# Hybrid encoder layer on one core: late gate products that share a weight unit between two blocks, and mLSTM exponents with a bias

## The chip, the cores and the metric

The kernel runs on one core of one Trainium2 chip. The metric is the device time of one execution in microseconds (us); three executions of the kernel before gave 2991.52, 2993.33 and 2995.25, median 2993.33. A difference under about 0.2% (6 us) can't be told from none.

## The reference, cut to what matters

One encoder layer on 2048 tokens of width 1024, all in float32. Three mixers run on the same normalised input `h`: a bidirectional chunked mLSTM (4 heads), a neighbourhood attention and a cross-attention; sigmoid gates computed from `h` merge them, an output projection and an MLP follow. The change touches the gates and the exponents of the mLSTM:

```python
gates = jax.nn.sigmoid(gate_pre)              # gate_pre = h @ w_in[:, 2576:5648], 3 x 1024 columns
y = (gates[:, :, 0] * (h_m @ w_proj_mlstm) + gates[:, :, 1] * (h_na @ w_proj_na)
     + gates[:, :, 2] * (h_mem @ w_proj_mem))
...
# one mLSTM chunk, one direction, one head; lf, ig: log forget gate and input gate per token
b = jnp.cumsum(lf)
d_log = jnp.where(tril, b[:, None] - b[None, :] + ig[None, :], -jnp.inf)
m_t = jnp.maximum(b + m_st, jnp.max(d_log, axis=-1))
s = (q @ k.T) * jnp.exp(d_log - m_t[:, None])
w_inter = jnp.exp(b + m_st - m_t)
```

The exponent of the chunk's 128 x 128 matrix is a sum of a number per query token (`r = b - m`) and a number per key token (`a = ig - b`).

## The kernel before, in words

Tokens stand in four blocks of 512. Every large product is three matmuls in a shortened float32 format (high by high, high by low, low by high), in the helper `mm3`, lines L232 to L234. In a product of channels by tokens (`ch_group`) a weight unit of 128 channels is the stationary operand, 8 pieces of the inner dimension follow one another, and 512 tokens are the moving columns: 24 matmuls. Weight units come from memory as 512 KB (`wr`, L172), ScalarE takes the high part (L176), VectorE the low part (L177), into one of five buffers `ws`; `take` fetches several units ahead, in the order of the list in `plan`.

- **Phase 1** makes the projections of the four blocks and both attentions; the gates of blocks 2 and 3 too. Its last products are the four of `o` in block 3 (destination `mm`, stationary operand `hT`). Between them the input operand `hT` of block 1 is copied back from memory into the place of block 3's, 128 tokens at a time; the last 128 tokens come in eight pieces (L568).
- **Phase 2**, the mLSTM stage, has 48 gate products left: 24 of block 1, then 24 of block 0 (`late_gates`, `gate`). Each fetches its own weight unit. Between the two blocks `hT` is loaded again (L609), and four ticks pass without a product.
- **Phase 3** merges, projects, and runs the MLP. Its operands are seven planes of one tile `X`.

A *tick* comes after every six matmuls of a gate product. At a tick the mLSTM stream `ml_stream` issues its next step, so the order on TensorE (PE) is written out by hand: six gate matmuls, one small mLSTM step, six gate matmuls. On the other engines a scheduler sets the order by priority; each engine then executes in order, and SyncE (SP) issues all transfers in one queue. The stream starts after 20 ticks. It alternates between the two directions, one chunk of 128 tokens each four ticks. Before the first chunk of a block of 512 tokens, `ml_block` computes that block's rows for one direction in one go: two scans on VectorE (L750, L754), differences, splits (L759 to L767), an exponential, four small transposes (L773). Scans and differences of a direction work on 4 partitions.

A chunk (`ml_chunk`) passes through steps: its loads; the exponents, by one matmul into PSUM (`pd`, L810) whose operands `at` and `rd` are built from the rows by VectorE and GpSimd (L807), an exponential on ScalarE (`de`, L812) and a mask on GpSimd (L814); the products of q and k (L828), masked by `de` into `pt` (L830); transposed keys (L839) and copies for the other direction (`sk`, L832, L841); outputs (`pn`, L863, L866); state update (`pu`, L872, into `C`, L878); and, for the direction that comes second to a chunk, normalisation, transposes `tr` (L905) and storage (`hm`, L907, L908). In the second half of the stage the copies in `sk` replace L828 and L839.

In phase 2 PSUM has two buffers for gate products (`mm`), four for `pn`, and two, called `mx`, that all other small results (`pd`, `psc`, `pk`, `pu`, `tr`) take in turn.

Of the kernel before, what the change touches and what calls it, by code (L numbers as in the profile page):

```python
# [16 lines left out]
ALU = mybir.AluOpType  # L17
# [8 lines left out]
TICKS_2, START_2 = 4, 20  # L26
PAD = 192
# [53 lines left out]
class Body:  # L81
# [176 lines left out]
    def phases(self):  # L258
# [7 lines left out]
        with tc.tile_pool(name="p2", bufs=1) as self.p_a:  # L266
            self.pad(self.p_a, PAD)
            self.ev_bufs = EV[2]
            self.psum(self.phase_2, mm=2, pn=4, mx=2)
        with tc.tile_pool(name="p3", bufs=1) as self.p_a:  # L270
            self.pad(self.p_a, PAD)
            self.ev_bufs = EV[3]
            self.psum(self.phase_3, mm=8)
# [14 lines left out]
    def scratch(self):  # L288
# [16 lines left out]
            w=[[d(f"s_w{i}{b}", [4, TB]) for b in range(NB)] for i in range(2)],  # L305
            hm=[d(f"s_hm{b}", [128, 2, 4, TB]) for b in range(NB)],
# [289 lines left out]
    def gate(self, b, j):  # L596

        p = self.ch_group(self.take(1)[0], self.hT)
# [4 lines left out]
    def late_gates(self, more):  # L603

        while self.gq and more():
            b, j = self.gq.pop(0)
            if j == 0 and b != GATES_2[0]:
                for k in range(0, 8, 2):
                    self.nc.sync.dma_start(self.hT[:, :, k:k + 2].bitcast(F32), self.scr["hT"][b][:, :, k:k + 2])  # L609
                for _ in range(TICKS_2):  # L610
                    self.tick()
            self.gate(b, j)


    def phase_2(self):
        nc, a = self.nc, self.a
        self.ml_consts()
# [6 lines left out]
    def ml_stream(self):  # L624


        for _ in range(START_2):
            yield
        dirs = [list(range(16)), list(range(15, -1, -1))]
        live = [[], []]  # L630
        when = {0: [(2, 0)], 1: [(1, 1), (2, 1), (3, 0)], 2: [(1, 2)], 3: [(3, 0), (1, 3), (0, 1)]}
        d = 0
        while any(dirs) or any(live[0]) or any(live[1]):
            c = dirs[d].pop(0) if dirs[d] else None
            if c is not None and c % 4 == (0, 3)[d]:
                self.ml_block(d, c // 4)
            live[d] = [None if c is None else self.ml_chunk(d, c)] + live[d][:3]
            for tick in range(4):
                for age, _ in when[tick]:
                    if age < len(live[d]) and live[d][age]:  # L640
                        next(live[d][age], None)
                yield
# [32 lines left out]
    def ml_consts(self):  # L675
# [7 lines left out]

        self.bd = t("bd", [36, 4, 128])
        nc.vector.memset(self.bd, 0.0)
        for d in range(2):
            nc.gpsimd.affine_select(out=self.bd, in_=self.bd, compare_op=ALU.not_equal, fill=1.0, base=-32 * d,
                                    pattern=[[-1, 4], [0, 128]], channel_multiplier=1)


        self.at, self.rd, self.rp = {}, {}, {}
        for d in range(2):
            for i in range(2):
                at = self.at[d, i] = t(f"at{d}{i}", [100, TB], F32R)
                rd = self.rd[d, i] = t(f"rd{d}{i}", [100, 4, 128], F32R)
                rp = self.rp[d, i] = t(f"rp{d}{i}", [36, TB])
                for x in (at, rd, rp):
                    nc.gpsimd.memset(x.bitcast(F32), 0.0)
                for k in range(2):
                    nc.vector.tensor_copy(rd[32 * k:32 * k + 4], self.bd[32 * k:32 * k + 4])  # L700
                    nc.vector.tensor_scalar(at[64 + 32 * k:68 + 32 * k], self.reset[32 * k:32 * k + 4], 0.0, 1.0, ALU.mult, ALU.add)
        self.carry = t("carry", [36, 1])
        nc.vector.memset(self.carry, NEG)
        self.packs = []
# [33 lines left out]
    def ml_block(self, d, b):  # L738

        nc = self.nc  # L740
        n = b if d == 0 else 3 - b
        hs = slice(32 * d, 32 * d + 4)
        if d == 0:
            self.packs.append({x: self.row("r_" + x, (36, TB + (x == "m")), bufs=1) for x in "ifbmw"})
        P = {x: y[hs] for x, y in self.packs[n].items()}
        ig, lf, bs, m, w = (P[x] for x in "ifbmw")
        nc.sync.dma_start(ig, self.scr["ig"][4 * d:4 * d + 4, b * TB:(b + 1) * TB])
        nc.sync.dma_start(lf, self.scr["lf"][4 * d:4 * d + 4, b * TB:(b + 1) * TB])
        rev = (lambda x: x[:, ::-1]) if d else (lambda x: x)
        nc.vector.tensor_tensor_scan(rev(bs), self.reset[hs], rev(lf), 0.0, ALU.mult, ALU.add)  # L750
        cm, ce = (m[:, 1:], m[:, 0:1]) if d == 0 else (m[:, :TB], m[:, TB:])
        carry = self.carry[hs]
        nc.vector.tensor_copy(ce, carry)
# [824 lines left out]
```

## Time and profile before

| | us |
|---|---|
| median of three runs | 2993.33 |
| the profiled execution, whole | 2998.03 |
| its span (first to last instruction) | 2996.3 |
| PE busy in the span | 2929.4 (98%) |
| VectorE (DVE), ScalarE (ACT), GpSimd (POOL) busy | 2066.5, 1195.8, 268.8 |
| phase 1, to the last product of `o` | 0 to 946.5 |
| phase 2 and the last gate products | 946.5 to 1377.3 |
| phase 3 | 1377.3 to 2996.3 |

Rows of PE in a timeline show an instruction's start and its modelled length, which overlaps with the next; what an instruction costs is the distance of two starts. A group's idle time is the time in which the engine stood still ahead of it, with what ended the wait.

### The profile page before, as it was taken

How to read it: one execution, taken by the hardware profiler on the slowest of the kernel's cores; microseconds unless marked ns; L12 is line 12 of the kernel's file. 1: busy time of each engine (PE TensorE's matmuls, PEld its weight loads, DVE VectorE, ACT ScalarE, POOL GpSimd, SP SyncE). 2: the span in 40 equal slices, each digit the busy share in tenths (PEclk: the TensorE clock that was granted, in tenths of full speed). 3: DMA queues.
4: the chain of work that ended last, by engine and by line, in shares of the span. 5: the costliest groups of instructions: out<-in, count | busy, mean ns of one | idle time of the engine just before them, and what ended most of it. 6: DMA issues, size and time to landing. Idle time of an engine off the chain costs nothing.

```text
span 2996.3 us, 41916 instructions
## 1 busy us (share of the span) xinstructions
PE 2929.4 (98%) x15028; PEld 2375.1 (79%) x15028; DVE 2066.5 (69%) x3523; ACT 1195.8 (40%) x2198; POOL 268.8 (9%) x423
## 2 busy tenths in 40 slices
PE   8999999999989899999999999999999999999999
PEld 6888888778777677778888888888778888888887
DVE  6676864476654766765688878666675987885665
ACT  6465654355543333342243333533312433334331
POOL 4121200021001323420000000000000000000000
PEclk9999999999999999999999999999999999999999
DMA  8786877876998667788444445766863444466554
GB/s 276 222 275 200 242 231 246 275 215 203 289 283 267 199 202 236 247 275 306 141 132 161 144 149 178 256 195 218 280 209 119 148 151 146 142 223 226 191 185 165
DMA packets 341712, 632.97 MB, mean 211 GB/s; under 512 B 29344, under 2 KB 151008, under 8 KB 341504
## 3 DMA queue, kind: packets, MB, share of 16 engines
q1 hardware_dynamic: 341504, 630.30, 65.5%
q8 instruction: 118, 1.93, 0.3%
q14 instruction: 90, 0.74, 0.1%
HBM read 453.63 MB, written 176.55 MB: 210 GB/s over the span
## 4 chain that ended last, share of the span: by engine, by line
PE 55%; DVE 2%; DMA 2%; issue 1%; ACT 0%; POOL 0%; SPq 0%; DVEq 0%; ACTq 0%; POOLq 0%
PE mm L232 18%; PE mm L233 18%; PE mm L234 18%; PE mm L1341 0%; DMA wr<-in_w_units_dram 0%; DMA hf<-s_hf 0%; DVE h L901 0%; DMA og<-s_o 0%; DVE ev L1497 0%; DVE acc L1490 0%; ACT hf L897 0%; POOL rs L325 0%; DMA X<-s_a 0%; DVE ws L177 0%; DVE h L889 0%
## 5 line engine op out<-in xcount | busy, mean ns | idle before, releaser
L232 PE MATMUL mm<-X,ws 128*128 128x512 f32 x1152 | 455.7, 396 | 0.0
L234 PE MATMUL mm<-X,ws 128*128 128x512 f32 x1152 | 455.4, 395 | 0.0
L233 PE MATMUL mm<-X,ws 128*128 128x512 f32 x1152 | 455.4, 395 | 0.0
L232 PE MATMUL mm<-hT,ws 128*128 128x512 f32 x896 | 375.0, 419 | 8.2 <-DMA hT<-s_hT 4.4
L177 DVE TENSOR_TENSOR ws<-wr,ws 128x1024 fp32r<-128x1024 f32 (+1 forms) x212 | 264.5, 1254 | 136.2 <-ACT ws L176 132.6
L234 PE MATMUL mm<-hT,ws 128*128 128x512 f32 x896 | 353.2, 394 | 0.0
L233 PE MATMUL mm<-hT,ws 128*128 128x512 f32 x896 | 353.2, 394 | 0.0
L233 PE MATMUL mm<-X 128*128 128x512 f32 x896 | 349.6, 390 | 3.4 <-DVE X L1464 3.4
L234 PE MATMUL mm<-X 128*128 128x512 f32 x896 | 349.3, 390 | 0.5 <-DVE X L1464 0.5
L232 PE MATMUL mm<-X 128*128 128x512 f32 x896 | 349.3, 390 | 0.0
L1463 ACT ACTIVATE X<-X 128x1024 fp32r<-128x1024 f32 x176 | 186.6, 1062 | 324.7 <-DMA X<-s_t 115.7
L1464 DVE TENSOR_TENSOR X<-X 128x1024 fp32r<-128x1024 f32 x176 | 214.6, 1224 | 136.7 <-ACT X L1463 135.8
L176 ACT ACTIVATE ws<-wr 128x1024 fp32r<-128x1024 f32 (+1 forms) x212 | 223.4, 1058 | 163.8 <-PE mm L234 88.9
L232 PE MATMUL mm<-ws,hT 128*128 128x512 f32 (+2 forms) x704 | 259.8, 369 | 2.7 <-ACT zif L524 1.8
L234 PEld LDWEIGHTS mm<-X,ws 128*128 128x128 f32 x1152 | 216.4, 188 | 52.3
L232 PEld LDWEIGHTS mm<-X,ws 128*128 128x128 f32 x1152 | 216.4, 188 | 52.2
L233 PEld LDWEIGHTS mm<-X,ws 128*128 128x128 f32 x1152 | 216.5, 188 | 52.1
L234 PE MATMUL mm<-ws,hT 128*128 128x512 f32 (+2 forms) x704 | 249.6, 355 | 2.0 <-DVE hT L434 2.0
L233 PE MATMUL mm<-ws,hT 128*128 128x512 f32 (+2 forms) x704 | 248.9, 354 | 0.0
L202 ACT ACTIVATE ws<-wr 128x512 fp32r<-128x512 f32 x224 | 135.1, 629 | 229.8 <-PE mm L234 148.8
L232 PEld LDWEIGHTS mm<-hT,ws 128*128 128x128 f32 x896 | 170.1, 190 | 49.7 <-issue 10.7
L234 PEld LDWEIGHTS mm<-hT,ws 128*128 128x128 f32 x896 | 169.6, 189 | 38.9
(266 smaller groups left out, 4865.8 us busy)
## 6 DMA issues: line engine op xcount, KB each, us to landing
wr<-in_w_units_dram SPq DMA_DIRECT2D x308, 512.0 KB
s_s<-u SPq DMA_DIRECT2D x32, 1024.0 KB
X<-s_s SPq DMA_DIRECT2D x64, 512.0 KB
X<-s_t SPq DMA_DIRECT2D x64, 512.0 KB
s_g<-ev SPq DMA_DIRECT2D x96, 256.0 KB
ev<-s_g SPq DMA_DIRECT2D x96, 256.0 KB
s_a<-u SPq DMA_DIRECT2D x96, 256.0 KB
X<-s_a SPq DMA_DIRECT2D x48, 512.0 KB
```

The costliest lines, as they stand in the source:

```text
L176: nc.scalar.activation(w[:, 0], raw, AF.Copy)
L177: nc.vector.tensor_tensor(w[:, 1], raw, w[:, 0].bitcast(F32), ALU.subtract)
L202: nc.scalar.activation(hi, src, AF.Copy)
L232: mm(out, lhs[0], rhs[0], start=first, stop=False)
L233: mm(out, lhs[0], rhs[1], start=False, stop=False)
L234: mm(out, lhs[1], rhs[0], start=False, stop=last)
L1463: nc.scalar.activation(hi, src, AF.Copy)
L1464: nc.vector.tensor_tensor(lo, src, hi.bitcast(F32), ALU.subtract)
```

## The change

Gates: 6 products of block 1 alone, then 18 weight units that serve block 1 and block 0 one after the other, then 6 of block 0 alone. Block 0's operand has a tile of its own, `hB`, loaded in the first ticks of the stage; the load between the blocks and its four ticks go. The very first product is computed for 384 tokens and then for the other 128. Units fetched in the stage: 30 in place of 48.

Exponents: `pd`, `at`, `rd`, `rp` go. The row `r` is stored to memory; each chunk loads it as `rb`, repeated over 128 partitions, and ScalarE computes `exp(rb + a)` with `a`, one number per partition, as bias, one instruction per head. `a` comes out of the block's small transposes, which are twice as many.

Rows: `ml_rows` computes both directions of a block step by step over ticks, ahead of need; three of the element-wise operations work on both directions at once. One step of the second direction's output (its normalisation) comes one tick earlier.

Memory: the pad of 192 bytes in each of two phases becomes one of 256 bytes ahead of both; `X` has five planes, and the other two share a buffer with `hB`.

```diff
-        for g in GATES_2:
-            out += u["gate"]
+        out += u["gate"] + u["gate"][:ALONE]                  # ALONE = 6
...
+        with tc.tile_pool(name="b", bufs=1) as self.p_b:
+            self.pad(self.p_b, PAD)                           # PAD = 256, was 192
...
-    def ch_group(self, w, rhs, ks=range(8)):
+    def ch_group(self, w, rhs, cuts=(0, TB)):
         p = self.ps("mm")
-        for k in ks:
-            self.mm3(p, (w[:, 0, k], w[:, 1, k]), (rhs[:, 0, k], rhs[:, 1, k]), k == ks[0], k == ks[-1])
-            if k % 2:
-                self.tick()
+        for c0, c1 in zip(cuts, cuts[1:]):
+            for k in range(8):
+                self.mm3(p[:, c0:c1], (w[:, 0, k], w[:, 1, k]), (rhs[:, 0, k, c0:c1], rhs[:, 1, k, c0:c1]), k == 0, k == 7)
+                if k % 2 and c0 == 0:
+                    self.tick()
...
     def phase_2(self):
+        hB = self.p_b.tile([128, 2, 8, TB], F32R, name="hB", tag="B", bufs=1)
+        load = lambda k: nc.sync.dma_start(hB[:, :, k].bitcast(F32), self.scr["hT"][GATES_2[1]][:, :, k])
+        self.jobs += [None] * 4
+        for k in range(8):
+            self.jobs += [lambda k=k: load(k), None]
...
-        self.gq = [(b, j) for b in GATES_2 for j in range(24)]
+        self.gq = [(0, j, True, whole) for j in range(ALONE)]
+        self.gq[0] = (0, 0, True, (0, CUT, TB))               # CUT = 384
+        for j in range(ALONE, 24):
+            self.gq += [(0, j, True, whole), (1, j, False, whole)]
+        self.gq += [(1, j, True, whole) for j in range(ALONE)]
...
     def ml_stream(self):
-        for _ in range(START_2):
+        rows = self.ml_rows(0)
+        for tick in range(START_2):                           # 20
+            if tick >= ROWS_2:                                # 8
+                next(rows, None)
             yield
...
-        when = {0: [(2, 0)], 1: [(1, 1), (2, 1), (3, 0)], 2: [(1, 2)], 3: [(3, 0), (1, 3), (0, 1)]}
+        when = {0: [(2, 0), (3, 0)], 1: [(1, 1), (2, 1)], 2: [(1, 2)], 3: [(3, 0), (1, 3), (0, 1)]}
...
-            if c is not None and c % 4 == (0, 3)[d]:
-                self.ml_block(d, c // 4)
+            if slot % 8 == 3 and slot < 24:
+                rows = self.ml_rows(slot // 8 + 1)
+            slot += 1
...
     def ml_rows(self, n):
+        for d, b, hs in dirs:
+            for x, name in ((lf, "lf"), (ig, "ig")):
+                nc.sync.dma_start(x[hs], self.scr[name][4 * d:4 * d + 4, b * TB:(b + 1) * TB])
+        for _ in range(4):
+            yield
+        for d, _, hs in dirs:
+            nc.vector.tensor_tensor_scan(rev(d, bs[hs]), self.reset[hs], rev(d, lf[hs]), 0.0, ALU.mult, ALU.add)
+            yield
...
+        nc.vector.tensor_tensor(a, ig, bs, ALU.subtract)
+        nc.vector.tensor_tensor(r, bs, cm, ALU.subtract)
+        for d, b, hs in dirs:
+            self.store(self.scr["r"][d][b].rearrange("c h t -> h c t"), r[hs].rearrange("h (c t) -> h c t", t=128))
...
     def ml_chunk(self, d, c):
+        rb = self.t(f"rb{d}", [128, 4, 128], 2)
+        nc.sync.dma_start(rb, self.scr["r"][d][b][cc].unsqueeze(0).to_broadcast([128, 4, 128]))
...
-        nc.gpsimd.tensor_tensor(rd[64:100], self.bd, R["rp"][:, cs].unsqueeze(1).to_broadcast([36, 4, 128]), ALU.mult)
         yield
-        pd = self.ps("mx", (128, 4, 128))
-        nc.tensor.matmul(pd, R["at"][:, cs], rd, start=True, stop=True)
         de = self.t(f"de{d}", [128, 4, 128], 1)
-        nc.scalar.activation(de, pd, AF.Exp)
+        for h in range(4):
+            nc.scalar.activation(de[:, h], rb[:, h], AF.Exp, bias=R["ac"][:, cc, h:h + 1])
...
     def phase_3(self):
-        X = self.p_a.tile([128, 7, 2, 4, TB], F32R, name="X")
+        X = self.p_a.tile([128, 5, 2, 4, TB], F32R, name="X")
...
+        B = self.p_b.tile([128, 2, 2, 4, TB], F32R, name="B", tag="B", bufs=1)
+        self.X.update(b21=B[:, 0], t4=B[:, 1])
```

In what follows lines of the kernel before keep their numbers; the same statements stand a few lines lower in the changed kernel (L828 becomes L837, L830 L839, L839 L848, L872 L881, L905 L914, L600 L603).

How the change moves instructions is shown at three places. The first is on PE in the second half of the stage, around one state update. Names ahead of the arrow are results, behind it operands; numbers tell buffers apart. Before:

```order
L866 MATMUL pn_14277<-C_2630_14096,qw_2640_14147 128x129
L234 MATMUL mm_14268<-hT,ws_13727 128x512
L810 MATMUL mx_14293<-rd_10780,at_10789 128x512
L872 MATMUL mx_14298<-v_2594_13936,kw_2639_14145 64x129 x4
L905 MATMUL tr_14342<-ident,h_2633_14105 128x128 x4
L234 MATMUL mm_14365<-hT,ws_13837 128x512
```

and now:

```order
L875 MATMUL pn_14287<-C_2607_14113,qw_2617_14160 128x129
L235 MATMUL mm_14278<-hT,ws_13193 128x512
L881 MATMUL mx_14313<-v_2572_13950,kw_2616_14158 64x129 x4
L914 MATMUL tr_14353<-ident,h_2610_14122 128x128 x4
L235 MATMUL mm_14371<-hB,ws_13193 128x512
```

Rows of gate matmuls that only repeat are left out. The exponents' matmul has gone from between the gate matmuls and the state update, so two results and not three share the two buffers `mx` here; and the two gate products around them use one weight unit, `ws_13193`.

The second is on DVE at the first two chunks, where the rows of the second block of 512 tokens are computed (`r_b`, `r_f`, `r_m`, `r_i`); the scans read SCALAR_TENSOR_TENSOR in it. Before:

```order
L830 TENSOR_TENSOR pt_1954_11140<-mx_11142,de_1953_11131 128x2x128
L750 SCALAR_TENSOR_TENSOR r_b_11633<-reset,r_f_11632 4x512
L845 TENSOR_TENSOR kw_1958_11162<-mx_11157,de_1953_11131 128x256
L754 SCALAR_TENSOR_TENSOR r_m_11634<-r_f_11632,r_m_11634,r_i_11631 4x512
L177 TENSOR_TENSOR ws_11112<-wr_11111,ws_11112 128x8x128
L755 COPY carry<-r_m_11634 4x1
L759 TENSOR_TENSOR r_i_11631<-r_i_11631,r_b_11633 4x512
L762 TENSOR_TENSOR r_b_11633<-r_b_11633,r_m_11634 4x512
L761 TENSOR_TENSOR at_10769<-r_i_11631,at_10769 4x512
L830 TENSOR_TENSOR pt_1968_11206<-mx_11207,de_1967_11197 128x2x128
```

and now:

```order
L839 TENSOR_TENSOR pt_1951_11142<-mx_11144,de_1950_11130 128x2x128
L178 TENSOR_TENSOR ws_11077<-wr_11076,ws_11077 128x8x128
L854 TENSOR_TENSOR kw_1955_11164<-mx_11159,de_1950_11130 128x256
L839 TENSOR_TENSOR pt_1965_11214<-mx_11215,de_1964_11202 128x2x128
L839 TENSOR_TENSOR pt_1965_11214<-mx_11216,de_1964_11202 128x2x128
L754 SCALAR_TENSOR_TENSOR r_b<-reset,r_f 4x512
L854 TENSOR_TENSOR kw_1969_11236<-mx_11231,de_1964_11202 128x256
L760 SCALAR_TENSOR_TENSOR r_m<-r_f,r_m,r_i 4x512
```

The scan that waits for its load (`r_f`) stood between the `pt` of chunk 0 and the `pt` of chunk 15, with the rest of the row work; it stands behind both now, ahead of the second `kw`.

The third is on ACT at the same place and a little later. Before:

```order
L812 ACTIVATE de_1967_11197<-mx_11195 128x512
L760 ACTIVATE at_10769<-r_i_11631 4x512
L763 ACTIVATE rp_10771<-r_b_11633 4x512
L832 ACTIVATE sk_1946_11101<-mx_11207 128x2x128
L832 ACTIVATE sk_1946_11101<-mx_11208 128x2x128
```

and now, two chunks on:

```order
L892 ACTIVATE sm_11286<-pn_11260 128x2
L821 ACTIVATE de_2001_11377<-rb_1973_11244,r_a_1933_11029 128x128
L841 ACTIVATE sk_1956_11166<-mx_11304 128x2x128
L841 ACTIVATE sk_1956_11166<-mx_11305 128x2x128
L177 ACTIVATE ws_11181<-wr_11180 128x8x128
L850 ACTIVATE sk_1956_11166<-mx_11323 128x256
```

The copies `sk` stood behind two instructions that need rows from DVE; they stand behind exponentials of a later chunk that need the load of `rb`.

More of the change, by code (lines that the diff above doesn't have):

```diff
@@ L605, in late_gates @@
         while self.gq and more():
[L606 to L612, printed above, removed]
+            i, j, new, cuts = self.gq.pop(0)
+            if new:
+                self.gw, = self.take(1)
+            self.gate(GATES_2[i], j, self.gw, self.h2[i], cuts)
     def phase_2(self):
         nc, a = self.nc, self.a
+        hB = self.p_b.tile([128, 2, 8, TB], F32R, name="hB", tag="B", bufs=1)
[3 more added lines that the diff above has]
+            self.jobs += [lambda k=k: load(k), None]
+        self.h2 = [self.hT, hB]
         self.ml_consts()
@@ L641, in ml_stream @@
                         next(live[d][age], None)
+                next(rows, None)
                 yield
@@ L682, in ml_consts @@
         nc.vector.memset(self.reset.rearrange("p (c t) -> p c t", t=128)[:, :, 0:1], 0.0)
[L684 to L701, printed above, removed]
         self.carry = t("carry", [36, 1])
         nc.vector.memset(self.carry, NEG)
-        self.packs = []
+        self.pack = [t("r_" + x, [36, TB + 2 * (x == "m")]) for x in "ifbmw"]
+        for x in self.pack:
+            nc.gpsimd.memset(x, 0.0)
         self.rows = {}
@@ new lines, in ml_rows @@
+        for d, b, hs in dirs:
+            yield
+            p = self.ps("mx", (128, 4, 128))
+            for c in range(4):
+                for x, col in ((cm, 0), (a, 4)):
+                    nc.tensor.transpose(p[:, c, col:col + 4], x[hs, c * 128:(c + 1) * 128], self.ident[hs, hs])
+            em, ac = self.row(f"r_em{d}", (128, 4, 4)), self.row(f"r_a{d}", (128, 4, 4))
+            nc.scalar.activation(em, p[:, :, 0:4], AF.Exp, scale=-1.0)
+            nc.vector.tensor_copy(ac, p[:, :, 4:8])
+            self.rows[d, b] = dict(em=em, ac=ac)
```

84 lines of the change are left out of this document (36 added, 48 removed).

## The prediction

> **What bounds the kernel now.** I read the page's totals first, then the busy time by stage, then PE's waits in the stage that the change touches, then the timeline at the longest of them.
>
> ```profile
> span 2996.3 us, 41916 instructions
> PE 2929.4 (98%) x15028; PEld 2375.1 (79%) x15028; DVE 2066.5 (69%) x3523; ACT 1195.8 (40%) x2198; POOL 268.8 (9%) x423
> 946.50:1377.30 430.80, 401.63 (x2188) 306.34 (x2187) 269.91 (x527) 159.59 (x418) 130.09 (x172) 0.98 0.74 238
> 1377.30:2996.30 1619.00, 1608.79 (x7041) 1311.21 (x7040) 1188.78 (x1641) 551.77 (x766) 0.00 (x0) 1.00 0.55 182
> ```
>
> The last two rows are stages: length, then busy time of PE, PEld, DVE, ACT and POOL, then clock, share of the DMA engines, GB/s. PE bounds the kernel. Phase 3 leaves 10.2 us of PE idle in 1619.0, the mLSTM stage 29.2 in 430.8; DVE is 63% busy there, ACT 37%, DMA 74%. So time can come from two places: PE work that goes, and the 29.2 us. These are listed in the waits of PE in the stage (sum, count, longest):
>
> ```profile
> PE mx L839 <- ACT sk L832: 7.4, 3, 5.9
> PE mm L232 <- DMA hT<-s_hT: 4.4, 1, 4.4
> PE mm L232 <- ACT ev L600: 3.8, 3, 1.9
> PE mx L872 <- DVE hm L908: 3.3, 5, 1.0
> PE tr L905 <- ACT de L812: 2.3, 1, 2.3
> PE mx L828 <- DVE kw L845: 2.2, 1, 2.2
> PE mx L828 <- ACT de L812: 2.0, 2, 1.0
> PE mx L810 <- ACT sm L883: 1.1, 1, 1.1
> ```
>
> These are 26.5 of the 29.2. None is a wait for a weight unit `ws`. The durations come from the profiled execution, 2998.03 us with a span of 2996.3; that is 0.16% above the median of 2993.33, and I take the differences over as they are.
>
> **Weight units once for two blocks: 0.** 18 fetches go: 18 times 512 KB, L176 and L177.
>
> ```profile
> L176 ACT ACTIVATE ws<-wr 128x1024 fp32r<-128x1024 f32 x48 | 50.8, 1057 | 57.0 <-DMA wr<-in_w_units_dram 40.9 <-PE mm L234 15.6 <-DMA wb<-s_w 0.3
> L177 DVE TENSOR_TENSOR ws<-wr,ws 128x1024 fp32r<-128x1024 f32 x49 | 63.2, 1291 | 45.4 <-ACT ws L176 42.4 <-DMA wb<-s_w 2.6
> L812 ACT ACTIVATE de<-mx 128x512 f32<-128x512 f32 x32 | 19.0, 593 | 32.3 <-PE mx L810 30.4 <-issue 1.6 <-POOL rs L324 0.2
> L897 ACT ACTIVATE hf<-h 128x128 f32<-128x128 f32 x64 | 19.0, 298 | 26.5 <-DVE h L894 26.5
> wr<-in_w_units_dram SPq DMA_DIRECT2D x48, 512.0 KB
> ```
>
> ACT loses 18 x 1.06 = 19 us, DVE 18 x 1.29 = 23 us, DMA 9.4 MB; all beside PE's products. The rows `rb` bring 32 x 256 KB = 8.4 MB back, and `hB` takes the place of the reload. The four ticks without a product go at no gain: PE had mLSTM steps there. PE computes the same 48 products.
>
> **First product in two pieces: -4.3 us.** PE's timeline at the start of the stage:
>
> ```profile
> 946.35 0.39 PE L234 MATMUL mm<-ws,hT 128*128 128x512 f32 x1
> 951.13 0.77 PE L232 MATMUL mm<-hT,ws 128*128 128x512 f32 x1 [4.39 <-DMA hT<-s_hT]
> 952.80 0.63 PE L232 MATMUL mm<-hT,ws 128*128 128x512 f32 x1
> 953.23 0.63 PE L233 MATMUL mm<-hT,ws 128*128 128x512 f32 x1
> 958.32 0.39 PE L232 MATMUL mm<-hT,ws 128*128 128x512 f32 x1
> ...
> 1274.15 0.60 PE L905 MATMUL tr<-ident,h 128*128 128x128 f32 x4
> 1274.51 0.48 PE L232 MATMUL mm<-hT,ws 128*128 128x512 f32 x1
> ```
>
> The product before starts its last matmul at 946.35, the second gate product starts at 958.32: with 0.23 for that matmul, the first gate product and its wait take 11.7. The last 128 tokens of `hT` are what is late. Matmuls after the wait stand 0.43 apart, not 0.23: PE runs slow for a while after standing still. Now 24 matmuls of 384 columns need no late tokens: 24 x 0.227 x 3/4 = 4.1, which covers 946.6 to 950.7. The other 24 of 128 columns are not in this trace; 128/512 of 0.227 is 0.057, a whole one 0.227, so 1.4 to 5.4 in all. I take 0.09, the spacing of the four 128-column transposes L905 (0.36 for 4): 2.2. The eight late copies leave SP until 951.4, so I add 1.1 for the last of them. 4.1 + 2.2 + 1.1 = 7.4.
>
> The Trainium skill, "TensorE: Matmul & The Clock Gate", Part 1 (The HAM clock gate), says that PE halves its clock after an idle window of about 3.4 us and takes about as long to recover; the 0.43 here agrees. By that rule a wait of 2.3 us would cost no slow stretch; the rows below at 1285.81 show one, so the trace decides, and short waits count with theirs.
>
> **Gate results late on ACT: -3.1.** Two of the three waits on L600 stand in the first 45 us:
>
> ```profile
> 965.18 0.50 PE L232 MATMUL mm<-hT,ws 128*128 128x512 f32 x1 [1.26 <-ACT ev L600]
> 989.98 0.50 PE L232 MATMUL mm<-hT,ws 128*128 128x512 f32 x1 [1.85 <-ACT ev L600]
> ```
>
> There ACT's queue waits behind setup on DVE and behind row splits (L760, L763) that wait for DVE. Setup of `at`, `rd` and `rp` and the splits go. The third stays.
>
> **No `pd`: -7.3 on PE, -10.2 in waits.** The matmul's price is the distance from the last gate matmul to it, since the state update behind it has the same lead either way:
>
> ```profile
> 1084.76 0.39 PE L234 MATMUL mm<-hT,ws 128*128 128x512 f32 x1
> 1084.98 0.39 PE L810 MATMUL mx<-rd,at 100*128 100x512 f32 x1
> 1085.30 0.66 PE L872 MATMUL mx<-v,kw 128*64 128x129 f32 x8
> ...
> 1285.81 1.11 PE L905 MATMUL tr<-ident,h 128*128 128x128 f32 x4 [2.34 <-ACT de L812]
> 1287.58 0.63 PE L234 MATMUL mm<-hT,ws 128*128 128x512 f32 x1
> 1288.01 0.63 PE L232 MATMUL mm<-hT,ws 128*128 128x512 f32 x1
> ```
>
> 32 x 0.227 = 7.3. With `pd`, three results share two `mx` buffers, and each waits until the one two places ahead has been read: L872 for `hm` (3.3), L905 and L828 for `de` (2.3, 2.0), L810 itself (1.1), together 8.7; without it the same buffer is freed a step earlier. The wait at 1285.81 also slowed what came behind it (0.43 apart): five matmuls by 0.2 each and the transposes by 0.4, 1.5 more with rounding.
>
> **Rows in steps: -8.9.** The longest wait of the stage, with DVE around it:
>
> ```profile
> 1017.98 0.69 PE L839 MATMUL mx<-ident,qk 128*128 128x128 f32 x2 [5.90 <-ACT sk L832]
> 1021.03 1.28 PE L863 MATMUL pn<-v,pt 128*128 128x129 f32 x5
> ...
> 1002.94 0.33 SPq L748 DMA_DIRECT2D r_f<-s_lf  x1
> 1008.20 1.21 DVE L750 TENSOR_TENSOR_SCAN r_b<-reset,r_f 4x512 f32<-4x512 f32 x1 [5.56 <-DMA r_f<-s_lf]
> 1017.08 0.76 DVE L830 TENSOR_TENSOR pt<-mx,de 128x256 f32<-128x256 f32 x2
> ```
>
> A scan stands in DVE's queue, waits 5.6 us for a load of 8 KB that was issued 5.3 us earlier, and the rest of the row work holds `pt` back until 1017.08; `sk` and PE's L839 wait for it. L839 7.4 and L828 on `kw` 2.2 are 9.6, the slow stretch behind them takes 3.05 us to 1021.03 for six gate matmuls and two transposes, 1.5 at full speed, and lasts into `pn`: 2.2 more. In the new order both `pt` stand ahead of the scan, and a second direction no longer follows at once. I take three quarters of 11.8, since a scan still stands ahead of the second `kw`.
>
> **What it adds.** 32 more transposes of rows, 4 columns wide: the L773 rows cost
>
> ```profile
> L773 PE MATMUL mx<-ident,r_m 4*128 4x4 f32 x32 | 3.2, 203 | 0.2 <-DVE C L878 0.2
> ```
>
> 0.1 busy each, and as L905's four stand 0.09 apart I take 0.08: +2.6. Four exponentials of 128 columns for one of 512: the nearest row, L897, takes 298 ns without a bias, so 4 x 0.3 = 1.2 against 0.59: 0.6 more a chunk on ACT, 19 us in all, against the 19 that L176 gives up and what L760 and L763 did. They wait for `rb` and no longer for `pd`, so they can start earlier; on the path 0. If that cover goes, they hold the `sk` copies behind them (first rival). On SP each `rb` stands ahead of the loads of `wb`, and everything behind it comes that much later; POOL's product for `qw` waits for `wb` and PE's `pn` for it. POOL gains the 32 L807. Bounds of these new waits: 0, and 12, two waits like the 5.9. I take 3, half of one, because one scan still waits for a load.
>
> Pad, addresses, `B`: no row shows an effect of an address. The same operations of phase 3 run beside PE, which stands still 10.2 us there; 0, with 3 either way. The merge at 1377.3 comes one gate product (5.4) sooner after the last chunk than before, since no ticks are lost between the blocks. The cover is this:
>
> ```profile
> 1353.22 1.74 SPq L1271 DMA_DIRECT2D X<-s_hm  x4
> 1360.01 4.15 SPq L1271 DMA_DIRECT2D X<-s_hm  x4
> ```
>
> The second row begins block 2's loads, so block 3's have left SP by 1360, 17 us ahead of their use; 5.4 less is still enough.
>
> **Sum:** -4.3 - 3.1 - 7.3 - 10.2 - 8.9 + 2.6 + 3 = -28.2. Median 2993.3 - 28.2 = 2965; the span of a profiled run about 2968.
>
> **Rivals.** *Exponentials on the path.* ACT executes in order, and in the new order exponentials of a later chunk stand among the `sk` copies. With 0.6 us more a chunk on the path, 32 x 0.6 = 19, the result is -9: 2984. ACT's 37% speaks against it. The Trainium skill, "ScalarE: Activation LUTs" (What ACT_TABLE_LOAD costs), gives an instruction with a pointer bias 280 ns plus 0.83 ns a column, less 93 ns between neighbours. By it four take an estimated 1.27 us and one without 0.61, the trace's 0.59; on the path that would be 21 us, 2986.
>
> *Loads of `rb` too late: slower.* The same copies wait when `rb` lands late. Between PE's L839 of one chunk and the next lie 24 gate matmuls, 5.4 us, and the small steps; `r_f` took 5.3 from issue to use, and `rb` is issued behind three other loads. It decides from 28.2/32 = 0.9 us lost a chunk; with 1.9, as much again, 2993 + 30 = 3023. For it: 74% DMA share, the 5.6 us wait. Against: `rb` is issued four ticks or more ahead.
>
> *The waits move.* The row work or the loads find other victims and half of the 22 us of waits comes back: -17, 2976, inside my range. *No gain:* the waits are all replaced and only `pd` and the first product count: -9, 2984.
>
> **Chances.** My forecast, 2955 to 2984: 0.74. Its low end has no new waits (-3), all the row waits gone (-2.9), the first product at its bound (-2) and the remaining small waits gone (-2); its high end is the first or the last rival. Below 2955: 0.08. 2984 to 2999: 0.12, a third of it still faster by over 0.2%. Slower by the `rb` rival: 0.06. So faster 0.86, same 0.08, slower 0.06.
>
> **What would show it.** PE's waits in the stage fall from 29 us to about 10, without L810; no wait on `hT` above 1.5; no matmuls 0.43 apart at 1018 and 1286; the stage takes about 403 us. Waits of L848 (formerly L839) on `sk` with `rb` ahead on ACT would show the rivals. I am wrong if phase 3 changes by over 3 us, or if new waits exceed 12.

## The result and the profile after

The changed kernel takes 2944.07 us (median of four runs, 2941.14 to 2950.89), the kernel before 2992.89 beside it: ratio 0.9839, 95% interval 0.9821 to 0.9858, 48.8 us less. I had forecast 2965 with 2955 to 2984: the direction was right, the gain 21 us larger than forecast, and outside the range. The profiled execution has a span of 2943.4 us and took 2945.09.

First the totals of the page, then the busy time by stage (length, PE, PEld, DVE, ACT and POOL, clock, share of the DMA engines, GB/s):

```profile
span 2943.4 us, 41858 instructions
PE 2895.3 (98%) x15052; PEld 2370.3 (81%) x15052; DVE 2005.5 (68%) x3471; ACT 1186.6 (40%) x2256; POOL 210.0 (7%) x382
```

```profile
0.00:944.60 944.60, 916.22 (x5802) 756.46 (x5802) 608.26 (x1355) 484.44 (x1014) 135.62 (x251) 0.99 0.80 250
944.60:1347.10 402.50, 394.46 (x2213) 304.87 (x2212) 213.56 (x476) 151.86 (x477) 74.42 (x131) 0.99 0.80 249
1347.10:2943.40 1596.30, 1584.60 (x7041) 1309.01 (x7039) 1183.64 (x1640) 550.30 (x765) 0.00 (x0) 1.00 0.56 185
```

The span is 52.9 us shorter. Of this, 28.3 lie in the mLSTM stage (430.8 to 402.5), where I had 28.2, and 22.7 in phase 3 (1619.0 to 1596.3), where I had 0. In phase 3 PE executes the same 7041 matmuls and its idle time hardly changes (10.2 to 11.7 us): it is busy 24.2 us less with the same work. The other 1.9 us lie in phase 1, which the change leaves alone; over all the profiles its length scatters between 939 and 951 us.

The waits of PE in the stage (sum, count, longest) fell from 29.2 us to 8.0:

```profile
PE tr L914 <- DVE hm L917: 2.6, 3, 2.2
PE mx L781 <- ACT sk L841: 2.1, 2, 1.0
PE mm L233 <- ACT ev L561: 0.7, 1, 0.7
PE mm L233 <- ACT ev L603: 0.7, 1, 0.7
PE mx L848 <- ACT sk L841: 0.7, 1, 0.7
PE mx L837 <- DVE C L885: 0.5, 1, 0.5
PE mm L234 <- DMA hT<-s_hT: 0.3, 1, 0.3
```

The prediction's last part asked for just this: no L810, no wait on `hT` above 1.5, about 10 us in all. It also said that it would be wrong if phase 3 changed by over 3 us, and phase 3 did.

Phase 3 shows its gain in the groups by line and shape: count, busy time, mean ns. First the kernel before, then the changed one. `mm<-X,ws` streams `X` past a weight unit; `mm<-X` has both operands in `X`.

```profile
L233 PE MATMUL mm<-X,ws 128*128 128x512 f32 x1152 | 455.4, 395 | 0.0
L233 PE MATMUL mm<-X 128*128 128x512 f32 x896 | 349.6, 390 | 3.4 <-DVE X L1464 3.4
```

```profile
L233 PE MATMUL mm<-X,ws 128*128 128x512 f32 x896 | 348.9, 389 | 0.0
L233 PE MATMUL mm<-X 128*128 128x512 f32 x600 | 233.5, 389 | 0.1
```

Two forms of one shape differed by 5 ns before, and differ no longer. Since the matmuls in the profile overlap, the distance of their starts, here called the pace, is what counts. On the timeline, in the same stretch of the feed-forward product, before and after (the rows left out are matmuls of the same kind without a gap):

```profile
1599.83 0.40 PE L232 MATMUL mm<-X,ws 128*128 128x512 f32 x1
...
1605.89 0.40 PE L234 MATMUL mm<-X,ws 128*128 128x512 f32 x1
```

```profile
1569.82 0.39 PE L235 MATMUL mm<-X,ws 128*128 128x512 f32 x1
...
1575.93 0.39 PE L235 MATMUL mm<-X,ws 128*128 128x512 f32 x1
```

Before, 26 steps take 6.06 us, 0.2331 each; after, 27 steps take 6.11, 0.2263 each. Over all neighbouring matmuls of this form the means are 233.3 and 226.7 ns. Three lines with 1152 each are 3456 matmuls (in the changed kernel 768 of them stream `B` in place of `X`, at the same 226.7); times 6.6 ns that is 22.8 us, the whole difference of phase 3. The clock is 1.00 in both.

### The profile page after: what moved, and what is told of

Read it like the earlier page. It is cut to its first block, busy times and chain, and to the rows that moved or that the text cites. A ratio compares the mean times of both kernels' runs of the same rounds, so it can differ in the third digit from the quotient of the medians.

```text
span 2943.4 us, 41858 instructions
## 1 busy us (share of the span) xinstructions
PE 2895.3 (98%) x15052; PEld 2370.3 (81%) x15052; DVE 2005.5 (68%) x3471; ACT 1186.6 (40%) x2256; POOL 210.0 (7%) x382
## 4 chain that ended last, share of the span: by engine, by line
PE 53%; DVE 1%; DMA 1%; issue 1%; ACT 0%; SPq 0%; POOL 0%; DVEq 0%; ACTq 0%
PE mm L233 18%; PE mm L234 18%; PE mm L235 18%; PE mm L1353 0%; DMA ev<-in_x_dram 0%; DMA wr<-in_w_units_dram 0%; DVE ev L1509 0%; DVE acc L1502 0%; DMA X<-s_a 0%; DVE ws L178 0%; DVE ev L1364 0%; DVE ev L1365 0%; DVE X L1359 0%; DVE ev L1331 0%; PE pn L872 0%
## 5 line engine op out<-in xcount | busy, mean ns | idle before, releaser
L233 PE MATMUL mm<-X,ws 128*128 128x512 f32 x896 | 348.9, 389 | 0.0
L235 PE MATMUL mm<-X,ws 128*128 128x512 f32 x896 | 348.6, 389 | 0.0
L234 PE MATMUL mm<-X,ws 128*128 128x512 f32 x896 | 348.6, 389 | 0.0
L178 DVE TENSOR_TENSOR ws<-wr,ws 128x1024 fp32r<-128x1024 f32 (+1 forms) x194 | 239.1, 1240 | 132.8 <-ACT ws L177 131.4
L233 PE MATMUL mm<-hT,ws 128*128 128x512 f32 (+1 forms) x712 | 293.8, 413 | 0.7 <-ACT ev L561 0.7
L234 PE MATMUL mm<-hT,ws 128*128 128x512 f32 (+1 forms) x712 | 278.4, 391 | 0.3 <-DMA hT<-s_hT 0.3
L235 PE MATMUL mm<-hT,ws 128*128 128x512 f32 (+1 forms) x712 | 278.6, 391 | 0.0
L177 ACT ACTIVATE ws<-wr 128x1024 fp32r<-128x1024 f32 (+1 forms) x194 | 204.2, 1057 | 121.7 <-PE mm L235 81.9
L235 PE MATMUL mm<-X 128*128 128x512 f32 x600 | 233.5, 389 | 0.5 <-DVE X L1476 0.5
L233 PE MATMUL mm<-X 128*128 128x512 f32 x600 | 233.5, 389 | 0.1
L234 PE MATMUL mm<-X 128*128 128x512 f32 x600 | 233.4, 389 | 0.0
L1475 ACT ACTIVATE X<-X 128x1024 fp32r<-128x1024 f32 x108 | 114.7, 1062 | 207.5 <-DMA X<-s_t 66.4
L233 PEld LDWEIGHTS mm<-X,ws 128*128 128x128 f32 x896 | 168.2, 188 | 35.1
L235 PEld LDWEIGHTS mm<-X,ws 128*128 128x128 f32 x896 | 168.2, 188 | 34.9
L234 PEld LDWEIGHTS mm<-X,ws 128*128 128x128 f32 x896 | 168.2, 188 | 34.6
L1476 DVE TENSOR_TENSOR X<-X 128x1024 fp32r<-128x1024 f32 x108 | 131.6, 1223 | 80.1 <-ACT X L1475 79.5
L1502 DVE TENSOR_TENSOR acc<-acc,mm 128x512 f32<-128x512 f32 x192 | 126.3, 684 | 68.7 <-PE mm L235 68.6
L235 PEld LDWEIGHTS mm<-hT,ws 128*128 128x128 f32 x712 | 134.2, 188 | 29.9
```

The source lines that it names most:

```text
L177: nc.scalar.activation(w[:, 0], raw, AF.Copy)
L178: nc.vector.tensor_tensor(w[:, 1], raw, w[:, 0].bitcast(F32), ALU.subtract)
L233: mm(out, lhs[0], rhs[0], start=first, stop=False)
L234: mm(out, lhs[0], rhs[1], start=False, stop=False)
L235: mm(out, lhs[1], rhs[0], start=False, stop=last)
L1475: nc.scalar.activation(hi, src, AF.Copy)
```

## The experiments

**Phase 3: where a tile begins.** Each tile of SBUF has a fixed address. The traces don't show it; what follows is worked out from the sizes of the tiles and pads that lie ahead, and only the distances between tiles are needed. Counted from `ws`, modulo 256 bytes, `X` begins at 192 before and at 0 after; the table below puts `ws` of these two kernels at 0. Four kernels, with edits cut to the lines that matter, tell addresses from the lighter engines and the split of `X`, and one kind of address rule from another.

```diff
 # a_pad192, the changed kernel
-PAD = 256
+PAD = 192
 # b_pad256, the kernel before
-PAD = 192
+PAD = 256
 # a_ws64, the changed kernel
-            self.pad(self.p_ws, 128)
+            self.pad(self.p_ws, 64)
 # a_pad384, the changed kernel
-PAD = 256
+PAD = 384
```

> The changed kernel with PAD back at 192, all else as it is: `X`, `B` and `hB` begin 192 bytes past a multiple of 256, the weight units `ws` on a multiple of 256. Theory of addresses: the matmuls of phase 3 that stream `X` or `B` past `ws` stand 233.3 ns apart as before, not 226.7; about 3440 of them, +22.8 us, and the second block's 24 gate products out of `hB` another 576 times 6.6 ns, +3.8: about 2971 us, phase 3 about 1619. Theory of lighter engines (phase 3 gained by `B` apart from `X`, or by less work around it, addresses count nothing): 2944 us, phase 3 1596.

> The kernel before with PAD 256 alone. Theory of addresses: phase 3 falls from 1619 to about 1596, the pace of `X` past `ws` from 233.3 to 226.7 ns, the mLSTM stage stays at about 431: 2993 - 23 = 2970 us. Theory of lighter engines: 2993, pace 233.3.

> The changed kernel with the pad ahead of the weight units 64 bytes instead of 128, PAD 256: `ws`, `hT`, `hB`, `X` and `B` all begin 192 bytes past a multiple of 256, so that their distance is as in the changed kernel and each one's own alignment as `X` had it before. If the distance of `X` and `ws` (modulo 256) counts: pace 226.7 ns, about 2944 us. If the alignment of the streamed tile itself counts: pace 233.3 ns in phase 3, about 2971 us, and more where the gates and phase 1 stream `hT`.

> The changed kernel with PAD 384: `X`, `B` and `hB` begin 128 bytes past a multiple of 256, `ws` on one. If 128 bytes are the grain that counts: pace 226.7 ns, 2944 us. If it is 256: pace 233.3 or between, about 2971 us.

Measured: the changed kernel with PAD 192, 2964.36 us (0.9906 of before, 0.9883 to 0.9929); the kernel before with PAD 256, 2967.45 (0.9924, 0.9903 to 0.9945). One number moves 20 to 23 us in either kernel. The other two ran once, 2938.02 and 2959.53, so that their pace says more than their total. The group of `X` past `ws` in the four kernels, in this order:

```profile
L233 PE MATMUL mm<-X,ws 128*128 128x512 f32 x896 | 354.0, 395 | 0.0
```

```profile
L233 PE MATMUL mm<-X,ws 128*128 128x512 f32 x1152 | 448.1, 389 | 0.0
```

```profile
L233 PE MATMUL mm<-X,ws 128*128 128x512 f32 x896 | 348.9, 389 | 0.0
```

```profile
L233 PE MATMUL mm<-X,ws 128*128 128x512 f32 x896 | 353.9, 395 | 0.0
```

| kernel | `ws` modulo 256 | `X` modulo 256 | distance of starts, ns | phase 3, us |
|---|---|---|---|---|
| before | 0 | 192 | 233.3 | 1619.0 |
| changed | 0 | 0 | 226.7 | 1596.3 |
| a_pad192 | 0 | 192 | 233.3 | 1622.2 |
| b_pad256 | 0 | 0 | 226.7 | 1593.4 |
| a_ws64 | 192 | 192 | 226.7 | 1596.4 |
| a_pad384 | 0 | 128 | 232.4 | 1615.3 |

The run a_ws64 decides between the rules: `X` begins where a slow kernel has it, but `ws` does too, and the pace is fast. So it is not the alignment of the streamed tile that counts, but its distance to the stationary one: 0 modulo 256 is fast, 128 and 192 are slow. `mm<-X` fits, fast in every kernel: both its operands lie in one tile whose planes are multiples of 256 apart. Why the distance counts is not shown.

Two things in the same traces limit the rule. Where `ws` is streamed past `X` or `B`, 384 matmuls, the pace hardly changes between the pads 256 and 192 (228.8 and 229.2 ns in the kernel before) and is 232.6 with 384, so it matters which of the two tiles lies ahead. And `hT` past `ws`, which by the sizes of the tiles lies at 0 as well, averages 230 ns in each of these kernels, in phases 1 and 2: the distance is not all that sets a pace.

**The stage: parts taken out of the changed kernel.** Its sum came out as forecast, so I took the parts back one by one.

```diff
 # first_whole
-        self.gq[0] = (0, 0, True, (0, CUT, TB))
 # keep_pd, in ml_chunk ahead of the exponentials
+        pd = self.ps("mx", (128, 4, 128))
+        nc.tensor.matmul(pd, self.hT[0:100, 0, 0, 0:128], self.hT[0:100, 0, 1], start=True, stop=True)
+        nc.scalar.activation(self.t("pdr", [128, 1], 2), pd[:, 0, 0:1], AF.Copy)
 # rows_once, in ml_stream
-            if slot % 8 == 3 and slot < 24:
-                rows = self.ml_rows(slot // 8 + 1)
+            if slot % 8 == 0 and 0 < slot < 32:
+                for _ in self.ml_rows(slot // 8):
+                    pass
 # own_units, in late_gates; plan() lists the shared units twice
-            if new:
-                self.gw, = self.take(1)
+            self.gw, = self.take(1)
```

> The changed kernel with its first gate product whole again instead of cut at 384 columns. My term: PE stands still again for the last copy of `hT`, and the slow stretch of 0.43 us spacing behind it returns: the way from the last `o` matmul to the second gate product grows from 8.2 back to about 11.7 us, stage and total +3.5 to +4.3, 2948 us. Rival: the 4 us come back out of later waits of the stage, total within 1 us of 2944.

> The changed kernel with a matmul of 100 rows by 512 columns per chunk put back into an `mx` buffer at the place where `pd` stood, read by one ACT instruction of one column; its result is used for nothing. My terms: 32 matmuls of 0.227 us, +7.3, and waits for a free `mx` buffer, +10.2: stage from 402 to about 420, total about 2961 us, with PE's waits in the stage up from 8 to 17 us or so. Rival (the buffers were not the cause, the setup and the one large exponential were): +7.3 alone, 2951 us, waits as they are.

> The changed kernel with the row work of blocks 1 to 3 done at once, in the slot in which it is needed (loads, scans and transposes in one go), not in steps five slots ahead. My term: DVE stands with a scan at the head of its queue for the load of `lf`, and PE waits for `pt` and `sk` behind it; +8.9 us, stage about 411, total 2953, a PE wait near 6 us at one of the three places. As both directions are now at one place, it may be twice that at worst, 2962. Rival (the loads land under other work): within 2 us of 2944.

> The changed kernel in which each of the 48 gate products fetches and splits its own weight unit again: 18 fetches more on SP, ACT and DVE, the order of products as changed. My term: 0, 2944 us, since ACT's 19 and DVE's 23 us stand beside PE's products. Rival (the relief of DVE, ACT and DMA is what shortened the waits of the chunks): PE's waits in the stage rise from 8 us by 5 to 15, 2949 to 2959 us.

| kernel | us, median | ratio to before, interval | stage in its profile, us |
|---|---|---|---|
| changed | 2944.07 | 0.9839 (0.9821 to 0.9858) | 402.5 |
| first_whole | 2947.52 | 0.9855 (0.9838 to 0.9873) | 401.7 |
| keep_pd | 2960.17 | 0.9893 (0.9876 to 0.9909) | 411.9 |
| rows_once | 2945.64 | 0.9847 (0.9832 to 0.9863) | 405.8 |
| own_units | 2965.82 | 0.9909 (0.9893 to 0.9924) | 421.2 |

The cut and the steps of the rows can't be told from nothing in the total. The matmul costs 16.1 us, of which the stage of its profile shows 9.4: PE is busy 6.1 us more there and idle 3.3 more. The largest of PE's waits in keep_pd is one for an `mx` buffer, as I had named it:

```profile
PE mx L884 <- DVE hm L920: 5.3, 6, 1.9
```

The surprise is own_units: 18 fetches, which I had at 0, cost 21.8.

**Transfer or splits?** A fetch is a load and two large instructions. Each alone:

```diff
 # units_split: the 18 shared products get a copy made in SBUF, no load
+            nc.scalar.activation(w[:, 0], old[:, 0].bitcast(F32), AF.Copy)
+            nc.vector.tensor_tensor(w[:, 1], old[:, 1].bitcast(F32), old[:, 1].bitcast(F32), ALU.max)
 # units_dma: 18 loads more, which nothing reads
+            nc.sync.dma_start(raw[:, :1024], self.a["w_units"][self.last_unit])
 # before_fewer: the kernel before, 18 products take the unit of the one ahead
+        if n < 6 or n >= 42 or n % 2 == 0:
+            self.gw, = self.take(1)
```

> The changed kernel, where the 18 shared products get a copy of their unit made from SBUF by one ACT and one DVE instruction of the size of a split, without a load from memory. If the work and the place in ACT's and DVE's queues is what 18 fetches cost: as with 48 fetches, 2966 us, stage 421. If it is the load that ACT waits for in order, or the transfer: 2944 to 2950 us.

> The changed kernel with 18 loads of 512 KB more, of the shared units a second time, which nothing reads: no splits. If the transfers (9.4 MB, SP's queue) are what 18 fetches cost: 2966 us, stage 421. If it is ACT and DVE: 2944 to 2948 us.

> The kernel before with 18 fetches fewer: of the 48 late gate products those from the 7th to the 42nd come in twos that use one weight unit, so 18 products are computed with a wrong unit (their gates are wrong); the order of all else is as before. My term (18 fetches beside PE's products cost nothing): 2992 us, stage 431 (423 to 431 as profiled). The theory that came from the run with 48 fetches in the changed kernel: 18 fetches cost 19 us in the stage, 2973 us, PE's waits in the stage down from 29 to about 17.

Loads alone give the whole loss, 2964.90 us (0.9910, 0.9892 to 0.9928); splits alone 2950.54 (0.9861, 0.9841 to 0.9880, which overlaps the changed kernel's). With the loads, other loads land late. The wait of ACT's exponentials for `rb` in the stage, in the changed kernel, with the 18 loads, and with 18 copies without a load:

```profile
ACT de L821 <- DMA rb<-s_r: 10.2, 4, 4.3
```

```profile
ACT de L830 <- DMA rb<-s_r: 47.4, 23, 4.3
```

```profile
ACT de L836 <- DMA rb<-s_r: 0.7, 1, 0.7
```

It is not `rb` alone. With the 18 loads ACT also waits for weight units, which took 2.0 us in the changed kernel, and DVE for `hf`, the first direction's output read back, for which it does not wait in the changed kernel:

```profile
ACT ws L186 <- DMA wr<-in_w_units_dram: 42.4, 15, 7.2
DVE h L912 <- DMA hf<-s_hf: 18.3, 10, 3.0
```

PE's waits rise from 8.0 to 24.0 us; the largest with the 18 loads:

```profile
PE tr L923 <- DVE h L919: 8.3, 11, 1.2
PE tr L923 <- DVE hm L926: 4.1, 2, 2.6
PE mx L846 <- DVE C L896: 3.0, 3, 1.2
```

Followed back in the trace, from each wait of PE to what ended it and on from there, 13.4 of the 24 us begin at a late load of `hf`, 3.3 at one of `wr` and 1.7 at one of `rb`. One of them, from the load of `hf` over ACT's sums of squares (L915) and POOL's root (L337) to the transposes:

```profile
1316.19 0.69 DVE L912 TENSOR_TENSOR h<-h,hf 128x512 f32<-128x512 f32 x1 [1.65 <-DMA hf<-s_hf]
1316.92 0.31 ACT L915 ACTIVATE hf<-h 128x128 f32<-128x128 f32 x1 [0.34 <-DVE h L912]
1319.61 0.35 DVE L919 SCALAR_TENSOR_TENSOR h<-h,rs,og 128x128 f32<-128x128 f32 x1 [1.10 <-POOL rs L337]
1320.02 0.65 PE L923 MATMUL tr<-ident,h 128*128 128x128 f32 x2 [1.08 <-DVE h L919]
```

So most of the long wait for `rb` is hidden from PE in this run, and the loss reaches PE mainly by another load that the 18 make late. In own_units DVE waits 10.9 us for `hf` and ACT 21.5 for the store of `hm`.

The kernel before, though, does not gain from 18 fetches fewer: 2994.22 us, ratio 1.0008 (0.9994 to 1.0022). So sharing units is worth nothing there; in the changed kernel, which has 8.4 MB of `rb` in the same queue, it is worth 21.8. That the bytes of `rb` make the difference is argued and not shown: no run has the 18 loads without `rb`.

> The changed kernel without the loads of `rb` (32 of 256 KB), the exponentials read a constant tile instead (the decay matrix is wrong). If the stage is held by its transfers now, as the 18 loads more that cost 20 us for 9.4 MB suggest: up to 18 us less, stage 385 to 395, total 2926 to 2935 us. If 9.4 MB more only pushed it over an edge: stage 398 to 403, total 2940 to 2946 us.

```diff
-        nc.sync.dma_start(rb, self.scr["r"][d][b][cc].unsqueeze(0).to_broadcast([128, 4, 128]))
+        rb = self.gml.rearrange("p (a b) -> p a b", b=128)
```

Without the 32 loads of `rb`: 2942.29 us (0.9849, 0.9820 to 0.9877), stage 396.0, no change that the total can show. The transfers stand at an edge, then: 9.4 MB more cost 21 us, 8.4 MB less bring at most a few.

**Parts taken out of the kernel before.**

```diff
 # before_nopd
-        nc.tensor.matmul(pd, R["at"][:, cs], rd, start=True, stop=True)
-        nc.scalar.activation(de, pd, AF.Exp)
+        nc.scalar.activation(de, self.gml.rearrange("p (a b) -> p a b", b=128), AF.Exp)
 # before_norows (nopd_norows: both; nopd_fewer: before_nopd and before_fewer)
-                self.ml_block(d, c // 4)
+                if c // 4 == 3 * d:
+                    self.ml_block(d, c // 4)
+                else:
+                    self.rows[d, c // 4] = self.rows[d, 3 * d]
```

> The kernel before without the matmul into `pd`: the exponential of a chunk reads a constant tile of SBUF of the same size (the decay matrix is wrong); POOL's product for `rd` and the row work stay. My terms: -7.3 of PE work and -10.2 of waits for `mx` buffers, 2975 us, stage about 413. By the run that put a matmul back into the changed kernel (stage +9.4): 2983 us, stage about 421.

> The kernel before without the matmul into `pd` and with 18 fetches fewer, both (decay matrix and 18 of the gates are wrong). Each alone was within its measurement of the kernel before. If each hides behind the other (work on PE and loads each enough to fill the stage): the stage falls to about 405 to 415 us, total 2970 to 2980. If something else holds the stage, the row work at the blocks' starts: stage above 424, total 2990 or more.

> The kernel before with the row work of blocks 1 to 3 left out: the later chunks use the rows of each direction's first block (their decay is wrong). My term for the rows was -8.9 us, most of it the wait of 5.9 at the first of the three places: 2983 us, stage from about 428 to about 419. If the row work stands before PE at every block's start, hidden there by the waits for `mx`: the same or less, above 2988.

> The kernel before without the matmul into `pd` and without the row work of blocks 1 to 3, both. Without the matmul alone the total stayed, and PE waited 5 us twice for a state update that stood on DVE behind row work. If those waits are what ate the matmul's 7 us and its waits: 2965 to 2973 us, stage 402 to 411 (rows -9, matmul -9 to -17). If not: no more than the rows alone give, 2983.

> The kernel before once more, for a second profile of it. The first has the mLSTM stage at 431 us; the kernel before with PAD 256 had 423, though nothing else of it differs. If the two lengths are scatter of one kernel: a stage between 420 and 432 us and a pace of 233.3 ns in phase 3. If PAD shortened the stage: 430 to 432 again.

> The changed kernel with the matmul per chunk put back and the row work of blocks 1 to 3 at once. Alone they made the stage 412 and 406 us, from 402. If the parts add: stage 415, total 2962 us. If the late rows cost PE more once the `mx` buffers are short, as in the kernel before: stage 420 to 428, total 2967 to 2975 us.

Rows left out: 2980.98 us, 0.9970 (0.9960 to 0.9981), 9.7 us, as my term of 8.9 had it. The matmul left out: nothing, 1.0010 (0.9999 to 1.0020); with fewer fetches 1.0012 (1.0001 to 1.0024); with the rows left out 1.0004 (0.9994 to 1.0014), so it even ate the rows' gain. In before_nopd PE has 32 matmuls fewer in the stage and is busy only 1.7 us less (401.63 before), at a granted clock of 0.96 where it was 0.98:

```profile
944.10:1371.80 427.70, 399.97 (x2156) 305.85 (x2155) 272.35 (x527) 160.75 (x419) 137.15 (x172) 0.96 0.74 238
```

0.02 of 428 us is 8.6 us (an estimate), more than the 7.3 that I had for the 32 matmuls. PE waits there about as long as before, 27.7 us, twice for 5 us at a state update that stands on DVE behind row work; PE, then DVE:

```profile
1088.84 1.19 PE L826 MATMUL mx<-qk 64*128 64x128 f32 x6 [4.88 <-DVE C L876]
...
1082.87 1.66 DVE L761 TENSOR_TENSOR at<-r_i,at 4x512 fp32r<-4x512 f32 x1
1084.56 1.10 DVE L767 TENSOR_TENSOR r_w<-r_b,r_m 4x512 f32<-4x512 f32 x1
...
1087.01 1.18 DVE L750 TENSOR_TENSOR_SCAN r_b<-reset,r_f 4x512 f32<-4x512 f32 x1
1088.12 0.57 DVE L876 SCALAR_TENSOR_TENSOR C<-C,wb,mx 128x129 f32<-128x129 f32 x2
```

That looked like the whole story, and nopd_norows should then have been fast. It was not, by a wait of its own, on PE and then on POOL:

```profile
1033.81 0.69 PE L840 MATMUL mx<-ident,qk 128*128 128x128 f32 x2 [9.65 <-ACT sk L833]
...
1023.52 8.59 POOL L810 TENSOR_TENSOR rd<-bd,rp 36x512 fp32r<-36x512 f32 x7
1032.19 0.64 POOL L815 TENSOR_SCALAR_AFFINE_SELECT de<-de 128x512 f32<-128x512 f32 x1
```

Seven products for `rd` run one after another on POOL, since nothing reads them any more and nothing holds them back; the mask of `de` waits behind them. In before_nopd they come up to four in a row (7.3 us at 1014.43), where the kernel before has at most two. So the kernels without the matmul brought in a fault that the change does not have, and they don't measure the matmul. What it is worth in the order of the kernel before stays open.

The second profile of the kernel before has 428.0 us in the stage (2992.41 us in all), the first 430.8; b_pad256, with the same stage but for the pad, 423.2. A stage of one profile is thus known to some 4 us either way. The changed kernel with the matmul and the rows at once takes 2953.74 us (0.9882, 0.9867 to 0.9896), stage 409.6: no more than with the matmul alone. The two together do not make the 428 of before; what else holds that stage was not found.

## Why the prediction was wrong in its size

- **Pad, addresses, `B`: 0, with 3 either way.** This is the step that failed: it measured -22.7 in the profile, and the pad alone -22.8 in the kernel before (2967.45 against 2990.24). I wrote that no row shows an effect of an address. A row did: `mm<-X,ws` at 395 ns beside `mm<-X` at 390, one shape, one stage, one clock. I took 0.227 us as the pace of every matmul and did not ask why 3456 of them stood 0.233 apart. That figure, taken seriously, bounds the term at 3456 x 6.6 ns = 23 us. The Trainium skill, "SBUF — State Buffer" (Operand start alignment), treats a start address as a matter of legality, and says that its runs timed nothing; here the distance of two start addresses is worth 0.8% of the kernel.
- **The sum of the stage, -28.2: measured -28.3.** The agreement to 0.1 is luck: a stage of one profile is known to 4 us, and the terms below came out otherwise one by one.
- **Weight units: 0.** Right in the kernel before (1.0008), wrong in the changed one (21.8 us). I had set the 9.4 MB that go beside the 8.4 MB that come, and priced the units at 0 by themselves; that holds in the kernel before and not in the changed one. Of my rival *loads of `rb` too late* the waits on ACT do appear without the sharing (47.4 us), but PE is held mostly by `hf`; the price is 21.8/32 = 0.7 us a chunk, where I had put 1.9 (and 1.9 x 32 - 28.2 gives 3026, not the 3023 I wrote).
- **First product: -4.3.** From the last `o` matmul to the second gate product: 11.7 before, 8.5 after, so -3.2. The two pieces run as worked out (24 x 0.17, then 3.35 with the last wait); what I left out is a wait of 0.74 for `ev` (L561) at the start. Undone it costs 3.5 us in total, inside the scatter.
- **Gate results late on ACT: -3.1.** The waits on this copy in the stage went from 3.8 to 0.7, so -3.1; L561's new 0.7 is counted with the first product.
- **No `pd`: -7.3 and -10.2.** Put back, it costs 9.4 in the stage of one profile and 16.1 in total, against 17.5. The work is near what I had (6.1 busy); its waits are 3.3 in that profile, so if the profile is typical I sized them too large, by up to 7 us.
- **Rows in steps: -8.9.** -9.7 when the row work is left out; 1.6 when it is done at once in the changed kernel, where PE then waits 4.5 us at one place. So the steps are not what brought most of it. The change also takes the splits for `at` and `rp` out of the row work; that was not tried alone.
- **Exponentials: 0 on the path.** Right: ACT has the room, 152 us of 402. One takes 392 ns, not the 298 of my nearest row, and 32 times four are busy for 42.4 us, 1.33 a chunk, not 1.2:

```profile
L821 ACT ACTIVATE de<-rb,r_a 128x128 f32<-128x128 f32 x128 | 42.4, 392 | 47.5 <-issue 19.2 <-DMA rb<-s_r 10.2 <-DVE sm L893 10.0
```

  The estimate from the Trainium skill, "ScalarE: Activation LUTs" (What ACT_TABLE_LOAD costs), was 1.27, nearer to it.
- **What it adds: +2.6 and +3.** The small transposes L781 follow one another at 0.06 us at full clock, so 32 more cost about 2 us; the 0.08 was near. They also wait 2.1 us for `sk`, inside my 3. I had no term for what follows the second of these waits, 6.8 us at half the clock, which cost about 3.4 (an estimate: half of 6.8). The wait, then the stretch with its clock of 0.50:

```profile
1097.29 0.22 PE L781 MATMUL mx<-ident,r_m 4*128 4x4 f32 x1 [1.05 <-ACT sk L841]
...
1098.50:1105.30 6.80, 6.80 (x25) 5.18 (x23) 0.60 (x2) 2.24 (x7) 0.63 (x1) 0.50 0.75 268
```

- **Short waits and the slow stretch.** I expected no matmuls 0.43 apart near 1286. The waits that I had seen there are gone, but another stands in the place, with the same stretch behind it:

```profile
1288.71 0.66 PE L914 MATMUL tr<-ident,h 128*128 128x128 f32 x4 [2.16 <-DVE hm L917]
...
1290.09 0.63 PE L233 MATMUL mm<-hB,ws 128*128 128x512 f32 x1
1290.52 0.63 PE L234 MATMUL mm<-hB,ws 128*128 128x512 f32 x1
```

Taken out of the changed kernel one at a time, the four parts cost 3.5 + 16.1 + 1.6 + 21.8 = 43 us, where the stage gained 28. They are not shares of a sum, and that my own terms added up to the right one is no proof of them. What each part of the change is worth to the stage stays open.

## What to carry to other kernels

Compare the start-to-start distance of matmuls of one shape in different places of the trace: where one form is slower than another at the same clock and without waits, ask early for the distance of its two operands' addresses, here modulo 256 bytes. Price a change that takes bytes away and brings others as one term, and measure a part both ways, taken out of the new kernel and put into the old, since each way hides behind other waits. An experiment that leaves out a reader must leave out what wrote for it too.

## What was not expected of the hardware

- The distance from the stationary tile to the streamed one moves the pace of 512-column matmuls: for `X` past `ws` 226.7 ns at 0 modulo 256 bytes, 232.4 at 128, 233.3 at 192. The Trainium skill, "TensorE: Matmul & The Clock Gate" (Wait — 56ns, not 53.3ns?), gives 215.7 ns for 512 columns; no form of this kernel averages that in these traces.
- Between 9.4 MB of loads more and none the stage loses 20 us at nearly the same share of the DMA engines (0.80 in both): the share does not tell how near the edge a stage is. The waits behind single loads do, and the longest of them (`rb`, 47 us on ACT) is not the one that reaches PE.
- In the changed kernel a wait of PE of 1.05 us was followed 1.2 us later by 6.8 us at a granted clock of 0.50; the same wait at 1017.58 was not.
